# Column tiles for the attention value sums: prompt in two halves, sample in four quarters, and another place for the sample sums

## The chip, the cores and the metric

The kernel runs on one core of one Trainium2 chip. The metric is device time in microseconds. Three runs of the kernel before took 2574.14, 2576.84 and 2580.19 us; the median is 2576.84 us. One more execution was recorded by the hardware profiler.

The engines are called as the profile calls them: PE is TensorE (matmuls), PEld its weight loads, DVE is VectorE, ACT is ScalarE, POOL is GpSimd, and SP is the queue that issues most of the transfers. PSUM is the memory that matmuls write.

## The reference, cut to what matters

The program is one inference step of a two-layer decoder trunk. It serves a prompt of 1024 tokens and a sample group of 8 sequences with 8 new tokens each, which share all weights. Everything is fp32. Layer 0 joins a causal convolution with "stick-breaking" attention (8 heads of width 64); layer 1 joins a short convolution and a pooling; a SwiGLU block follows each.

The change touches only the end of the attention, the last line here:

```python
z = einsum('nqhd,nkhd->nhqk', qblk, k) * scale + bias_f
mask = k_pos[None, :] < pblk[:, None]
log_1m = where(mask, log_sigmoid(-z), 0.0)
after = cumsum(log_1m, reverse=True) - log_1m
wgt = exp(where(mask, log_sigmoid(z) + after, -inf))
out = einsum('nhqk,nkhd->nqhd', wgt, v)
```

For the prompt the keys are the prompt itself, so a query block of 128 tokens needs the key blocks up to its own. For the sample each of the 8 sequences has 8 pages of 128 past keys, found through a page table, and its 8 new keys.

## The kernel before, in words

**Main work and background work.** The order of instructions is written out by hand. The main work is the large matmuls of projections and SwiGLU (`mm3`, line 235: fp32r operands split into a high and a low part, three products). Between them stand slots; each slot calls `bg()` (line 341), which advances one background generator to its next `yield`. The attention and the convolution are such generators. One slot in the first SwiGLU is followed by 6 matmuls of 512 columns. Every engine takes its instructions in the order in which they were written.

**Tokens.** Prompt tokens 0 to 511 form group GA; prompt tokens 512 to 1023 and the 64 sample tokens form GB.

**Prompt attention** (`attention`, line 937) runs once for each group. Its units are pairs of head and query block: for GA the blocks 3, 2, 1, 0 of each head, for GB the blocks 7, 6, 5, 4. A unit passes four steps in four successive iterations of one loop (line 1029):

- s1: score matmuls into the PSUM tile `z2`, and two sigmoids on ACT (line 987).
- s2: on DVE two scans (lines 996 and 999) and a product (line 1001), which give the weights `be`.
- s3: PE transposes the weights, one 128x128 block per key block (line 1011), and ACT copies them into `wt` (line 1012).
- s4: the value sum. For key blocks 0 to i, a matmul adds a 64x128 product into one PSUM tile `o` (line 1020), and ACT copies it into the queries' place `qall` (line 1021).

An iteration u issues s4 of unit u-3, s3 of u-2, s2 of u-1, (in GB a slot,) s1 of u, then up to two small pieces that prepare the next head's keys and queries (lines 959 to 965), and a slot. The value rows `vrow` come from memory by one transfer a head (line 969).

**Sample attention** (`sample`, line 1051) takes two sequences at a time (`bp`, 4 of them). It has 48 steps: each handles half of the heads of up to three key pages. A step s transposes the key pages of step s+1 in two parts (`trans`, line 1104; PE line 1115, ACT line 1118, DVE line 1119), and multiplies the scores of step s (`score`, line 1128, line 1138). After the last page of a pair, the weights are made on DVE (lines 1163 to 1173) over the next three steps, then transposed in two parts (`weights_t`, line 1187): the first at once, the second through the list `soon`, and that of the new keys with the first value sum.

The value sums (`pv`, line 1202) wait in the list `pvq`, two pages of each sequence in one entry. The tile `o` has a half of 64 rows for each of the two sequences: 8 heads by 8 queries. A matmul with 64 weight columns adds all 512 value columns into such a half, so that each head's rows get the values of all heads; the useful blocks are picked at the end by `fin` with the selection matrix `sel` (line 1224). The value pages come by two transfers of 256 KB for each `pv` (line 597 through `page_to`); the tile `vst` has two buffers, so a page pair is loaded once the one two before it has been used.

In a step, the two parts of `trans` are separated by a `yield`; another `yield` stands before the scores, and a third at the end. An entry of `pvq` is taken after the scores in each even step, and in every step after the 48th.

**Two things at once in the sample stage.** `flow_c` (line 1358) interleaves `sample` with the second convolution `conv_b`: a `yield 1` of the sample attention leaves the convolution out, and of the other yields every second one advances it, by two DVE steps of 0.75 us.

Of the kernel before, what the change touches and what calls it, by code (L numbers as in the profile page):

```python
# [8 lines left out]
F = mybir.dt.float32  # L9
FR = mybir.dt.float32r  # L10
I32 = mybir.dt.int32
AF = mybir.ActivationFunctionType
OP = mybir.AluOpType
# [44 lines left out]
def trunk_kernel(ctx, tc, x_prompt, x_sample, cache_k, cache_v, state_conformer, state_shortconv, state_pool,  # L58
# [4 lines left out]
    pe, act, dve, pool, sp = nc.tensor, nc.scalar, nc.vector, nc.gpsimd, nc.sync  # L63
# [14 lines left out]
    def tmp():  # L78
        return tmpbox[0].tile([128, tmpbox[1]], F, name="tmp")
# [142 lines left out]
    def w_next(live=0):  # L222
        j = wj[0]
        wj[0] += 1
        w_split(j + 3 - live)
        w_load(need(j + 6 - live))
        return hls.pop(j)
# [411 lines left out]
    def ms():  # L639
        return mp.tile([128, 512], F, name="m")  # L640
# [5 lines left out]
    qall = hb[:, 4:8]  # L646
# [31 lines left out]
    m = ms()  # L678
# [258 lines left out]
    def attention(g):  # L937
# [3 lines left out]
        with ExitStack() as es_:  # L941
            pa = es_.enter_context(tc.tile_pool(name=f"pa{g.c0}", bufs=1))
            zp = es_.enter_context(tc.tile_pool(name=f"zp{g.c0}", bufs=1, space=PSUM, side="right"))
            op_ = es_.enter_context(tc.tile_pool(name=f"op{g.c0}", bufs=1, space=PSUM, side="right"))
# [4 lines left out]
            kt_, qa, vrow, small = {}, {}, {}, []  # L949
# [64 lines left out]
            def s4(u):  # L1014
                h, i = units[u]
                hp, hh = divmod(h, 2)
                w = wt.pop(u)
                o = op_.tile([64, 128], F, name="o2")
                for j in range(i + 1):
                    pe.matmul(o, vrow[h][:, j], w[:, j], start=j == 0, stop=j == i)  # L1020
                act.activation(qall[hh * 64:hh * 64 + 64, hp, i * 128:i * 128 + 128], o, AF.Copy)

            load_v(0)
            operands(0)
# [4 lines left out]
            for u in range(len(units) + 3):  # L1029
# [8 lines left out]
                if u < len(units):  # L1038
                    h, r = divmod(u, 4)
# [11 lines left out]
    def sample():  # L1051
# [5 lines left out]
        with ExitStack() as es_:  # L1057
            sa = es_.enter_context(tc.tile_pool(name="sa", bufs=1))
            zp = es_.enter_context(tc.tile_pool(name="zps", bufs=1, space=PSUM, side="right"))
            op_ = es_.enter_context(tc.tile_pool(name="ops", bufs=1, space=PSUM, side="right"))  # L1060
# [13 lines left out]
            for i in range(2):  # L1074
                r = slice(64 * i, 64 * i + 64)
                act.activation(sel[r, :, i], ident[r, r].rearrange("p (h x) -> p h x", h=4), AF.Copy)
            vnew = sa.tile([128, 512], F, name="vnew")
# [13 lines left out]
            vst, nv = {}, [0]  # L1091

            def load_v(upto):
                while nv[0] < min(upto, 32):
                    i = nv[0]
                    nv[0] += 1
                    bp, k = divmod(i, 8)
                    vst[i] = sa.tile([128, 2, 512], F, name="vst", bufs=2)
                    for b2 in range(2):
                        page_to(vst[i][:, b2], cache_v, (2 * bp + b2) * 8 + k)  # L1100
# [3 lines left out]
            def trans(u, pr, i):  # L1104
                bp, kb, b2 = units[u]
                n = (3, 3, 2)[kb]
                j = (2 * bp + b2) * 8 + 3 * kb
                if i == 0:
                    load_k(kpages.index(j) + n)
                    kth[u, pr] = sa.tile([128, 2, 2, 384], FR, name="kth", bufs=2)  # L1110
                t = kth[u, pr]
                if True:
                    m = ms()
                    for pg in range(n):
                        pe.transpose(m[:, pg * 128:pg * 128 + 128],
                                     kst[j + pg][:, (2 * pr + i) * 128:(2 * pr + i) * 128 + 128], ident)
                    h = t[:, 0, i, :n * 128]
                    act.activation(h, m[:, :n * 128], AF.Copy)
                    dve.tensor_tensor(t[:, 1, i, :n * 128], m[:, :n * 128], f32(h), op=OP.subtract)
                if i and pr:  # L1120
                    load_k(kpages.index(j) + n + KP)
                if i and kb == 2:
                    b = 2 * bp + b2
                    new = knew[:, 2 * pr:2 * pr + 2, 8 * b:8 * b + 8]
                    act.activation(t[:, 0, :, 256:264], new, AF.Copy)
                    dve.tensor_tensor(t[:, 1, :, 256:264], new, f32(t[:, 0, :, 256:264]), op=OP.subtract)

            def score(u, pr):
                bp, kb, b2 = units[u]
                if pr == 0:  # L1130
                    z[u] = zp.tile([128, 512], F, name="z")
                t = kth.pop((u, pr))
                n = NB[kb]
                for i in range(2):
                    hp = 2 * pr + i
                    q = qb[:, b2, hp * 128:hp * 128 + 128]
                    for s in range(2):
                        pe.matmul(z[u][:, :n], q, t[:, s, i, :n], start=hp == 0 and s == 0, stop=hp == 3 and s == 1)
# [19 lines left out]
            wx, wts, osum = {}, {}, {}  # L1158
# [34 lines left out]
            def turned(bp):  # L1193
                first, new = weights_t(bp)
                pvs = [lambda i=i: (pv(i), pv(i + 1)) for i in range(8 * bp, 8 * bp + 8, 2)]
                pvs[0] = lambda f=pvs[0]: (f(), new())
                soon.extend(first)
                pvq.extend(pvs)
# [3 lines left out]
            def pv(i):  # L1202
                bp, k = divmod(i, 8)
                if k == 0:
                    osum[bp] = op_.tile([128, 512], F, name="o")
                o = osum[bp]
                load_v(i + 1)
                for b2 in range(2):
                    r = slice(64 * b2, 64 * b2 + 64)
                    pe.matmul(o[r], wts[bp][:, k, r], vst[i][:, b2], start=k == 0, stop=False)  # L1210
                vst.pop(i)
                load_v(i + 3)
                if k < 7:
                    return
                for b2 in range(2):
                    r = slice(64 * b2, 64 * b2 + 64)
                    pe.matmul(o[r], wts[bp][:, 8, r], vnew, start=False, stop=True)
                ob = tmp()[:, 0:512]
                act.activation(ob, o, AF.Copy)

                def fin():
                    m = ms()
                    for hp in range(4):
                        pe.matmul(m[:, hp * 32:hp * 32 + 32], ob[:, hp * 128:hp * 128 + 128],
                                  sel[:, hp].rearrange("p b x -> p (b x)"), start=True, stop=True)
                    mv = m[:, 0:128].rearrange("p (h b y q) -> p h b y q", h=4, b=2, y=2)
                    c0 = SEQ + 16 * bp
                    for hh in range(2):
                        r = slice(hh * 64, hh * 64 + 64)
                        act.activation(qall[r, :, c0:c0 + 16].rearrange("p h (b q) -> p h b q", b=2),  # L1230
                                       mv[r, :, :, hh], AF.Copy)
                fins.append(fin)

            load_k(KP)
            steps = [(u, pr) for u in range(len(units)) for pr in range(2)]
            chain = {}
            pvq, soon = [], []
# [7 lines left out]
            s = 0  # L1245
            while s < len(steps) or chain or pvq or fins:
                todo = fins[:] + chain.pop(s, [])
                fins.clear()
                for f in todo:
                    f()  # L1250
                if s + 1 < len(steps):
                    trans(*steps[s + 1], 0)
                if s < len(steps):
                    yield 1 if todo else 2
                if s + 1 < len(steps):
                    trans(*steps[s + 1], 1)
                while soon:
                    soon.pop(0)()
                if s < len(steps):
                    yield 2  # L1260
                if s < len(steps):
                    u, pr = steps[s]
                    bp, kb, b2 = units[u]
                    score(u, pr)
                    if pr:
                        score_b(u)
                    if (kb, b2, pr) == (2, 1, 1):
                        if bp < 3:
                            fill_q(bp + 1)
                        w = weights(bp)  # L1270
                        for d, f in ((1, lambda w=w: next(w)), (2, lambda w=w: next(w)),
                                     (3, lambda bp=bp: weights_b(bp))):
                            chain.setdefault(s + d, []).append(f)
                        chain.setdefault(s + (4 if bp < 3 else 5), []).append(
                            lambda bp=bp: turned(bp))
                if pvq and (s % 2 == 0 or s >= len(steps)):
                    pvq.pop(0)()
                s += 1
                yield 2

# [372 lines left out]
    b2 = [xp.tile([128, 2, GB.n], FR, name=f"b2_{k}") for k in range(4)]  # L1653
# [67 lines left out]
    for n in range(2, KC):  # L1721
        h = w_next()
        a = accs()
# [4 lines left out]
    with tc.tile_pool(name="fab", bufs=1) as ep:  # L1728
        gen = forms_a(ep)
        for n in range(KC):  # L1730
            h = w_next()
            a = accs()
# [256 lines left out]
```

## Time and profile before

| What | us |
|---|---|
| Median of three runs | 2576.84 |
| Profiled execution | 2575.97 |
| Its span (first to last instruction) | 2574.2 |
| PE busy in it | 2477.7 |
| DVE busy in it | 1693.0 |
| ACT busy in it | 1105.3 |
| POOL busy in it | 1564.2 |
| Prompt value sums, first and last start | 238.2 and 563.7 |
| Sample value sums, first and last start | 679.4 and 924.4 |

Busy times overlap, since the engines run side by side. A row of a timeline gives the start, the length from the first start to the last end of the instructions merged in it, the engine, the line, the operation, the tile written and the tiles read, the shape and the count; then the idle time of the engine before it, and what ended that. A group row gives the busy time of the group and the mean length of one instruction, then idle time and what ended it. Matmuls are pipelined, so the length of one is longer than the distance of two starts.

### The profile page before, as it was taken

What the parts mean: (1) busy time and instruction counts of PE and PEld (TensorE: products, weight loads), DVE (VectorE), ACT (ScalarE), POOL (GpSimd) and SP (SyncE); (2) the same over time, 40 slices, a digit from 0 to 9 for tenths busy, and PEclk for the clock granted to TensorE, in tenths of its full rate; (3) what the DMA queues carried; (4) which work ended last, traced back from release to release, by engine and by line L of the source; (5) the groups of instructions that cost most, each with busy time, mean ns of one, the idle gap of its engine ahead of it and who ended that gap; (6) DMA issues with size and microseconds to landing.
All of it is one profiled execution on the core that took longest, in us unless ns stands there. A gap on an engine that the chain in (4) does not pass through costs nothing.

```text
span 2574.2 us, 41142 instructions
## 1 busy us (share of the span) xinstructions
PE 2477.7 (96%) x15727; PEld 2213.7 (86%) x15727; DVE 1693.0 (66%) x2359; ACT 1105.3 (43%) x1875; POOL 1564.2 (61%) x1205
## 2 busy tenths in 40 slices
PE   8999999999999999999999999999999998999998
PEld 6788877887777668989999889989888887999997
DVE  3696777968867734467666633348776778666655
ACT  5536766754444334334333522234434434443333
POOL 6754243544434346678777722266888885887775
PEclk9999999999999999999999999999999999999999
DMA  7342231224555434222323411152233332333322
GB/s 220 113 113 74 64 109 46 70 83 142 157 162 160 139 107 152 74 74 83 99 83 98 130 42 46 38 161 65 84 91 96 95 96 82 107 95 103 99 83 78
DMA packets 355484, 258.30 MB, mean 100 GB/s; under 512 B 22913, under 2 KB 303617, under 8 KB 355272
## 3 DMA queue, kind: packets, MB, share of 16 engines
q1 hardware_dynamic: 355256, 255.66, 33.8%
q8 instruction: 125, 2.05, 0.3%
q14 instruction: 71, 0.58, 0.1%
q10 hardware_dynamic: 32, 0.01, 0.0%
HBM read 237.41 MB, written 18.69 MB: 99 GB/s over the span
## 4 chain that ended last, share of the span: by engine, by line
PE 44%; DVE 8%; POOL 2%; issue 1%; ACT 1%; POOLq 0%; DVEq 0%; ACTq 0%
PE acc L235 23%; PE acc L521 20%; POOL hl L197 1%; DVE sum L200 1%; DVE hid L241 1%; DVE hb L295 1%; DVE sum L201 1%; DVE b L1669 0%; DVE tmp L525 0%; DVE sum L202 0%; DVE x L1669 0%; DVE sum_c L214 0%; DVE fb L1673 0%; DVE xs L1673 0%; POOL tmp L500 0%
## 5 line engine op out<-in xcount | busy, mean ns | idle before, releaser
L186 POOL TENSOR_TENSOR hl<-stage,hl 128x512 fp32r<-128x512 f32 x464 | 634.7, 1391 | 475.1 <-ACT hl L184 357.0
L235 PE MATMUL acc<-x,hl 128*128 128x512 f32 (+1 forms) x3648 | 780.6, 350 | 12.2 <-DVE hb L295 2.6
L235 PEld LDWEIGHTS acc<-x,hl 128*128 128x128 f32 x3648 | 581.4, 189 | 77.2 <-issue 10.9
L235 PE MATMUL acc<-hid,hl 128*128 128x288 f32 (+1 forms) x3096 | 552.3, 334 | 16.8 <-DVE hb L295 6.9
L235 PEld LDWEIGHTS acc<-hid,hl 128*128 128x128 f32 x3096 | 470.4, 190 | 69.9 <-DVE hb L295 11.0
L295 DVE TENSOR_TENSOR hb<-acc,hb 128x512 f32<-128x512 f32 (+1 forms) x360 | 256.4, 718 | 184.8 <-PE acc L235 183.4
L521 PE MATMUL acc<-x,hl 128*128 128x288 f32 (+1 forms) x2676 | 362.4, 290 | 6.0 <-ACT x L1792 2.0
L521 PEld LDWEIGHTS acc<-x,hl 128*128 128x128 f32 x2676 | 349.0, 188 | 8.4 <-POOL hl L197 2.7
L197 POOL TENSOR_TENSOR hl<-sum,hl 128x512 fp32r<-128x512 f32 x180 | 237.1, 1344 | 168.6 <-ACT hl L196 168.5
L184 ACT ACTIVATE hl<-stage 128x1024 fp32r<-128x1024 f32 x232 | 243.5, 1055 | 218.5 <-PE acc L235 129.6
L525 DVE TENSOR_TENSOR tmp<-acc,tmp 128x288 f32<-128x288 f32 (+1 forms) x420 | 173.5, 441 | 228.0 <-ACT tmp L537 135.3
L197 POOL TENSOR_TENSOR hl<-stage,hl 128x512 fp32r<-128x512 f32 x180 | 267.0, 1505 | 13.3 <-ACT hl L196 13.3
L521 PE MATMUL acc<-b,hl 128*128 128x256 f32 (+1 forms) x1548 | 216.6, 291 | 14.1 <-DVE tmp L525 11.2
L521 PEld LDWEIGHTS acc<-b,hl 128*128 128x128 f32 x1548 | 202.3, 189 | 19.6 <-ACT hl L196 12.7
L235 PE MATMUL acc<-x1t,hl 128*128 128x288 f32 x1152 | 216.4, 296 | 1.5 <-POOL hl L186 1.5
L235 PEld LDWEIGHTS acc<-x1t,hl 128*128 128x128 f32 x1152 | 196.0, 188 | 19.4 <-POOL hl L186 1.7
L196 ACT ACTIVATE hl<-sum 128x512 fp32r<-128x512 f32 x180 | 103.1, 623 | 237.9 <-DVE sum L202 217.6
L291 DVE TENSOR_TENSOR tmp<-acc,rr 128x512 f32<-128x512 f32 (+1 forms) x108 | 75.0, 709 | 113.2 <-PE acc L235 100.0
L500 POOL TENSOR_TENSOR tmp<-tmp 128x576 f32<-128x576 f32 (+1 forms) x85 | 127.8, 1504 | 11.7 <-ACT tmp L477 8.3
L196 ACT ACTIVATE hl<-stage 128x512 fp32r<-128x512 f32 x180 | 105.6, 618 | 67.5 <-PE acc L235 62.3
L241 DVE TENSOR_TENSOR hid<-tmp,hid 128x512 fp32r<-128x512 f32 (+1 forms) x88 | 99.1, 1127 | 44.0 <-ACT hid L240 41.2
L235 PE MATMUL acc<-x1a,hl 128*128 128x512 f32 x480 | 121.7, 407 | 2.5 <-POOL hl L186 1.3
(289 smaller groups left out, 3242.9 us busy)
## 6 DMA issues: line engine op xcount, KB each, us to landing
stage<-in_w_ffn_in_dram SPq DMA_DIRECT2D x176, 512.0 KB
stage<-in_w_ffn_out_dram SPq DMA_DIRECT2D x88, 512.0 KB
stage<-in_w_in_even_dram SPq DMA_DIRECT2D x40, 512.0 KB
kst<-in_cache_k_dram SPq DMA_DIRECT2D x64, 256.0 KB
vst<-in_cache_v_dram SPq DMA_DIRECT2D x64, 256.0 KB
stage<-in_w_out_even_dram SPq DMA_DIRECT2D x16, 512.0 KB
stage<-in_w_in_odd_dram SPq DMA_DIRECT2D x16, 512.0 KB
stage<-in_w_out_odd_dram SPq DMA_DIRECT2D x16, 512.0 KB
```

The source lines that it names most:

```text
L184: act.activation(hl[:, 0], st, AF.Copy)
L186: pool.tensor_tensor(hl[:, 1, c], st[:, c], f32(hl[:, 0, c]), op=OP.subtract)
L196: act.activation(hl[:, 0, c], x, AF.Copy)
L197: pool.tensor_tensor(hl[:, 1, c], x, f32(hl[:, 0, c]), op=OP.subtract)
L200: todo = [lambda: dve.tensor_tensor(sb, su[:, lo], su[:, hi], op=OP.add), lambda: dve.tensor_tensor(sa[:, hi], sg[:, lo], su[:, lo], op=OP ...
L235: pe.matmul(acc[:, b, :c1 - c0], w, xs[:, xi, c0 - o:c1 - o], start=first and s == 0, stop=last and s == 2)
L241: (on or dve).tensor_tensor(dst[:, 1], src, f32(dst[:, 0]), op=OP.subtract)
L291: dve.tensor_tensor(d, a, r, op=OP.mult)
L295: dve.tensor_tensor(d, a, d, op=OP.add)
L500: (dve if both and f == NF - 1 else pool).tensor_tensor(t[:, :n], t[:, :n], u[:, :n], op=OP.mult)
L521: pe.matmul(acc[:, :w2], h[:, wi, i, k], xk[:, xi], start=k == 0 and s == 0, stop=k == 3 and s == 2)
L525: dve.tensor_tensor(out, acc[:, :w2], x, op=OP.add)
```

## The change

In the prompt attention, the tile `o` gets 128 rows. The matmuls of even key blocks add into rows 0 to 63, those of odd key blocks into rows 64 to 127. Where there is more than one key block, ACT copies the upper half into a new tile `ot`, and DVE adds the lower half to it and writes the result; with one key block, ACT copies the lower half as before.

In the sample attention, each 64-row half of `o` becomes two quarters of 32 rows (four heads each), and a matmul for a quarter takes only the 256 value columns of its four heads. `o` becomes 256 columns wide, and so does the copy of it.

In the steps of the sample attention, an entry of `pvq` is taken between the two parts of `trans`, in odd steps (and in every step after the 48th), and not while `soon` holds something. The `yield` between the two parts of `trans` is kept only in steps that had other things to do first; otherwise it moves behind the second part.

```diff
-                o = op_.tile([64, 128], F, name="o2")
+                o = op_.tile([128, 128], F, name="o2")
                 for j in range(i + 1):
-                    pe.matmul(o, vrow[h][:, j], w[:, j], start=j == 0, stop=j == i)
-                act.activation(qall[hh * 64:hh * 64 + 64, hp, i * 128:i * 128 + 128], o, AF.Copy)
+                    pe.matmul(o[j % 2 * 64:j % 2 * 64 + 64], vrow[h][:, j], w[:, j], start=j < 2, stop=j >= i - 1)
+                r = slice(hh * 64, hh * 64 + 64)
+                a = qall[r, hp, i * 128:i * 128 + 128]
+                if i == 0:
+                    act.activation(a, o[0:64], AF.Copy)
+                    return
+                t = pa.tile([128, 128], F, name="ot", bufs=2)
+                act.activation(t[r], o[64:128], AF.Copy)
+                dve.tensor_tensor(a, o[0:64], t[r], op=OP.add)
...
-                    osum[bp] = op_.tile([128, 512], F, name="o")
+                    osum[bp] = op_.tile([128, 256], F, name="o")
...
-                for b2 in range(2):
-                    r = slice(64 * b2, 64 * b2 + 64)
-                    pe.matmul(o[r], wts[bp][:, k, r], vst[i][:, b2], start=k == 0, stop=False)
+                for t in range(4):
+                    r, c = slice(32 * t, 32 * t + 32), slice(256 * (t % 2), 256 * (t % 2) + 256)
+                    pe.matmul(o[r], wts[bp][:, k, r], vst[i][:, t // 2, c], start=k == 0, stop=False)
...
-                for b2 in range(2):
-                    r = slice(64 * b2, 64 * b2 + 64)
-                    pe.matmul(o[r], wts[bp][:, 8, r], vnew, start=False, stop=True)
-                ob = tmp()[:, 0:512]
+                for t in range(4):
+                    r, c = slice(32 * t, 32 * t + 32), slice(256 * (t % 2), 256 * (t % 2) + 256)
+                    pe.matmul(o[r], wts[bp][:, 8, r], vnew[:, c], start=False, stop=True)
+                ob = tmp()[:, 0:256]
...
-                        pe.matmul(m[:, hp * 32:hp * 32 + 32], ob[:, hp * 128:hp * 128 + 128],
+                        pe.matmul(m[:, hp * 32:hp * 32 + 32], ob[:, hp % 2 * 128:hp % 2 * 128 + 128],
...
                     trans(*steps[s + 1], 0)
-                if s < len(steps):
-                    yield 1 if todo else 2
+                if pvq and not soon and (s % 2 or s >= len(steps)):
+                    pvq.pop(0)()
+                if todo and s < len(steps):
+                    yield 1
                 if s + 1 < len(steps):
                     trans(*steps[s + 1], 1)
                 while soon:
                     soon.pop(0)()
                 if s < len(steps):
+                    if not todo:
+                        yield 2
                     yield 2
...
-                if pvq and (s % 2 == 0 or s >= len(steps)):
-                    pvq.pop(0)()
                 s += 1
                 yield 2
```

## The prediction

> **What bounds the kernel now.** I read the page first, its totals and its slices.
>
> ```profile
> span 2574.2 us, 41142 instructions
> PE 2477.7 (96%) x15727; PEld 2213.7 (86%) x15727; DVE 1693.0 (66%) x2359; ACT 1105.3 (43%) x1875; POOL 1564.2 (61%) x1205
> PE   8999999999999999999999999999999998999998
> DVE  3696777968867734467666633348776778666655
> ```
>
> TensorE is busy in every slice, so a matmul taken away shortens the run unless another engine then sets the pace. Slices 4 to 15 (64.4 us each) hold what the change touches, and there VectorE's digits go up to 9. So I asked for the stages: prompt attention of the first token half, of the second half, one head of the latter, sample attention, and its tail.
>
> ```profile
> core 0: us, PE busy (x) PEld busy (x) DVE busy (x) ACT busy (x) POOL busy (x), PEclk, DMA share, GB/s
> 238.25:337.10 98.85, 96.61 (x691) 85.05 (x690) 69.56 (x104) 67.90 (x156) 25.68 (x46) 1.00 0.22 60
> 359.00:564.00 205.00, 199.70 (x1164) 162.67 (x1164) 167.79 (x154) 134.85 (x217) 90.71 (x82) 1.00 0.21 58
> 474.39:498.33 23.94, 23.94 (x144) 19.74 (x143) 20.88 (x19) 16.88 (x28) 9.59 (x12) 1.00 0.20 55
> 565.00:900.00 335.00, 319.37 (x1560) 245.14 (x1558) 258.99 (x427) 136.44 (x281) 141.22 (x108) 0.99 0.53 155
> 900.00:930.00 30.00, 26.32 (x89) 11.70 (x90) 6.05 (x10) 6.45 (x13) 4.98 (x4) 0.94 0.50 140
> ```
>
> TensorE ends last in all of them, but in the second-half head VectorE works 20.88 of 23.94 us: it has 3.06 us of room for a whole head. In the sample stage it has 76 us of room in 335, and there the main work binds through TensorE alone.
>
> **Prompt value sums: what is removed.** The groups by shape give counts and prices.
>
> ```profile
> L1020 PE MATMUL o<-wt,vrow 128*64 128x128 f32 x576 | 76.6, 278 | 0.0
> L1210 PE MATMUL o<-vst,wts 128*64 128x512 f32 x128 | 39.3, 657 | 3.0 <-DMA vst<-in_cache_v_dram 1.6 <-ACT wts L1188 1.3
> L1217 PE MATMUL o<-vnew,wts 128*64 128x512 f32 x16 | 5.0, 596 | 0.0
> L1021 ACT ACTIVATE hb<-o 64x128 f32<-64x128 f32 x64 | 17.0, 266 | 35.6 <-PE o L1020 35.2
> L1149 DVE TENSOR_TENSOR zs<-z,zs 64x384 f32<-64x384 f32 x16 | 8.7, 546 | 4.4 <-ACT zs L1148 4.2
> ```
>
> An fp32 matmul leaves two records: 288 matmuls (8 heads x (4+3+2+1) and 8 x (8+7+6+5)) make 576. The mean of 278 ns is a latency; the pace is read off the timeline of TensorE.
>
> ```profile
> 480.60 1.74 PE L1020 MATMUL o<-wt,vrow 128*64 128x128 f32 x14
> 482.27 0.88 PE L1011 MATMUL m<-ident,be 128*128 128x128 f32 x6
> 492.57 1.31 PE L1020 MATMUL o<-wt,vrow 128*64 128x128 f32 x10
> 493.81 1.09 PE L1011 MATMUL m<-ident,be 128*128 128x128 f32 x8
> ```
>
> 14 records take 1.67 us to the next line's start, 10 take 1.24: 0.108 us each and about 0.15 of entry and exit, which stay. Whether two column halves run at once is shown by the sample sums, which use halves already:
>
> ```profile
> 721.11 0.64 PE L1138 MATMUL z<-kth,qb 128*128 128x264 f32 x4
> 721.68 0.20 PEld L1210 LDWEIGHTS o<-vst,wts 128*64 128x64 f32 x4
> 721.68 1.94 PE L1210 MATMUL o<-vst,wts 128*64 128x512 f32 x8
> 722.16 0.14 PEld L1210 LDWEIGHTS o<-vst,wts 128*64 128x64 f32 x2 [0.28 <-issue]
> 723.45 1.03 PE L1217 MATMUL o<-vnew,wts 128*64 128x512 f32 x4
> 724.41 1.66 PE L235 MATMUL acc<-x,hl 128*128 128x512 f32 x6
> ```
>
> Eight records of 512 columns take 1.77 us, 0.22 each; at the pace of the 128-column ones alone (0.108 x 4) one would take 0.43. So halves do run in pairs, and their weight loads come in pairs too (two in 0.14 us). With pairs, n matmuls take the time of n/2 rounded up: 4, 3, 2, 1 become 2, 2, 1, 1 (4 fewer a head) and 8, 7, 6, 5 become 4, 4, 3, 3 (12 fewer). Each is two records, 0.217 us: first half 8 x 4 x 0.217 = 6.9 us, second half 8 x 12 x 0.217 = 20.8, together 27.7.
>
> [...]
>
> **Prompt: what is added.** ScalarE's copy stays one of 64x128 (0.266 us), now of the upper half. New is a VectorE add for 56 of the 64 units. No add of 64x128 is in the trace; the 64x384 add from PSUM takes 0.546, the copy of this very shape on ScalarE 0.266, so between these; I take 0.28, near the copy, since the size is the same: 56 x 0.28 = 16 us of VectorE. Four a head make 1.1 us of the 3.06 of room, while TensorE takes 2.6 out of the head: 23.94 - 2.6 = 21.3 against 20.88 + 1.1 = 22.0. So VectorE becomes the bound by its work alone and 0.7 of the 2.6 is lost.
>
> More is lost to order. The add stands on VectorE ahead of the next unit's scans (line 996), and waits for ScalarE's copy, which waits in its own queue. A second-half head, by ScalarE, VectorE and TensorE:
>
> ```profile
> 511.60 1.05 ACT L959 ACTIVATE kt<-kall 64x1024 fp32r<-64x1024 f32 x1
> 512.56 0.61 ACT L960 ACTIVATE qa<-hb 64x512 fp32r<-64x512 f32 x1
> 513.08 0.25 ACT L1021 ACTIVATE hb<-o 64x128 f32<-64x128 f32 x1
> 510.60 1.54 DVE L996 TENSOR_TENSOR_SCAN q<-q,ident 128x128 f32<-128x128 f32 x1 [1.14 <-ACT q L987]
> 514.39 1.23 DVE L1001 TENSOR_TENSOR be<-be,q 128x1023 f32<-128x1023 f32 x1
> 517.74 1.09 PE L1011 MATMUL m<-ident,be 128*128 128x128 f32 x8
> ```
>
> The copy (behind the next head's key and query copies) ends at 513.33; the scan that now starts at 510.60 will start after it and the add, 3.0 us later. Its product, ready at 515.62, is needed by the transposes at 517.74: 2.1 us of slack, less the 1.1 that two shortened sums take out before it. That is 2.0 us of new TensorE wait in a head that saves 2.6; behind the scans stand VectorE's key subtractions and accumulator reads, so the following unit is late too. Such a head keeps almost nothing. First half:
>
> ```profile
> 277.37 0.41 DVE L996 TENSOR_TENSOR_SCAN q<-q,ident 128x128 f32<-128x128 f32 x1
> 278.22 0.27 ACT L1021 ACTIVATE hb<-o 64x128 f32<-64x128 f32 x1 [0.52 <-PE o L1020]
> 279.47 1.23 DVE L1001 TENSOR_TENSOR be<-be,q 128x255 f32<-128x255 f32 x1
> 281.23 0.44 PE L1011 MATMUL m<-ident,be 128*128 128x128 f32 x2
> ```
>
> Here the scan goes from 277.37 to 278.3 at the earliest (the copy comes 0.4 sooner, the add follows): 1.0 late against a slack of 281.23 - 280.70 = 0.5. Ends: the first half keeps 0 to 6.9, the second 0 to 20.8 less the 0.7 x 8. Not every head is like these two; nearer to the zero they show, I take 2 and 7: **9 us**.
>
> **Sample value sums.** A page pair's sum is now two pairs of 512-column records, 2 x 0.43 = 0.86 us (the 1.77 is two sums with the entry); it becomes 8 records of 256 columns in four quarters. No 32-column tile is in the trace. Ends: all four at once, 2 x 0.215 = 0.43; two at a time, 0.86; one after the other, 1.72. Halves run fully in pairs, so I take 0.44: 0.42 saved, for 24 sums and 3 closing ones before the tail: **11.3 us**. The evacuation (line 1219) halves, off the path. [...]
>
> **One fp32 clump.** The pop of the value sums moves from behind the scores to between the two transposes of the next step. Its page loads on SP's queue move with it, still ahead of that step's second key load, and each waits for its sum as before. From L1138 to L1210 TensorE takes 721.68 - 721.11 = 0.57 for four records that were issued at about 0.12, so some 0.1 is lost on entry. The new neighbours, full-width transposes, still change the column width; so between 0 and 12 clumps x 0.1 = 1.2 I take less than half, **0.5 us**. The slots for main work per step stay three. The convolution's VectorE pieces cover the two adjacent transposes' reads; if VectorE were full, each step could cost the 0.55 of such a read.
>
> **Tail.** The last eight sums:
>
> ```profile
> 900.68 1.09 PE L1187 MATMUL m<-ident,bet 128*128 128x128 f32 x8 [2.65 <-DVE bet L1173]
> 903.04 3.49 PE L1210 MATMUL o<-vst,wts 128*64 128x512 f32 x8 [1.27 <-ACT wts L1188]
> 905.08 14.28 SPq L597 DMA_DIRECT2D vst<-in_cache_v_dram  x12
> 923.07 0.64 PE L1210 MATMUL o<-vst,wts 128*64 128x512 f32 x1 [0.98 <-DMA vst<-in_cache_v_dram]
> 924.93 1.66 PE L235 MATMUL acc<-x,hl 128*128 128x512 f32 x6
> ```
>
> The first pop now comes one step after its weights, so main work covers the 1.27 us wait; the 2.65 stays. From 905 the value pages set the pace, and halved matmuls only free buffers a little sooner. Ends 1 and 7; I take 1.3 + 1.7 = **3 us**.
>
> **Sum.** 9 + 11.3 + 0.5 + 3 = 23.8. The profiled execution took 2575.97 us (span 2574.2); 2552.2 from it, and the median of the runs, 2576.84, lies 0.9 above: 2553.
>
> **Rivals.**
> A: the adds cost nothing, because VectorE and ScalarE have more slack elsewhere. For it: only 4 units a head, and TensorE waited little for line 1001 until now. Against: 20.88 of 23.94. 27.7 + 11.3 + 0.5 + 3 = 42.5: 2534.
> B: quarters run two at a time. Nothing excludes it in the trace. 9 + 0 + 0.5 + 1.5 = 11: 2566.
> C: at 128 columns the halves don't overlap, since a load of 0.136 us no longer fits under a stream of 0.108. Prompt then -3 (adds without a gain): 11.8 saved, 2565. [...]
> D, slower: the adds' wait ahead of line 996 falls on TensorE each time. From 42.5 / 56 = 0.76 us per add it eats all gains. At the delays of the two heads (1.3 for 24 adds, 3.0 for 8, 0.28 for 24) it would be 62 us: 19 slower, 2596. Against: slacks of 0.5 and 2.1 in the same rows.
>
> **Chances.** Forecast 50, A 17, B 12, C 11, D 5; no change to be told 5. The likeliest's own range is 2543 to 2562 (prompt 0 to 18). With A, B and C inside, 2533 to 2569. A measurement of this kernel tells about 0.2% (5 us) from no change: faster 0.89, same 0.05, slower 0.06.
>
> **What would show it.** L1020: the x14 clump at about 1.0 us instead of 1.67 (C: unchanged). L1210: eight records in 0.44 us, their loads in fours (B: 0.86). New TensorE waits "L1011 <- DVE L1001" of 10 to 20 us (A: under 5; D: over 45). The wait of 1.27 us for line 1188 gone. The prediction is wrong if such waits come from elsewhere, above all if adjacent transposes make TensorE wait for line 1119.

## The result, and the profile after

The changed kernel takes 2585.01 us (median of five runs, 2583.41 to 2590.14) against 2576.84: a ratio of 1.0036, 95% interval 1.0021 to 1.0050. It is slower by about 9 us; 24 us faster had been forecast. The page of its profiled execution:

```profile
span 2581.6 us, 41528 instructions
PE 2443.3 (95%) x15871; PEld 2194.4 (85%) x15871; DVE 1706.5 (66%) x2415; ACT 1106.4 (43%) x1875; POOL 1566.6 (61%) x1205
PE   8999888889999989999999999999999999999998
DVE  3696777787888845467666733347777778667655
```

TensorE has 34.4 us less work than before (2477.7), and the span is 7.4 us longer. The slices with an 8 for PE (5 to 9, where the kernel before has 9) are the prompt attention. So the matmul time was saved, and more than that came back as waiting. Stage by stage, first the changed kernel (prompt sums, sample stage), then the one before, each from the first prompt sum:

```profile
239.47:583.00 343.53, 297.88 (x1940) 241.94 (x1937) 265.83 (x332) 223.94 (x403) 124.04 (x136) 0.97 0.23 64
583.00:916.00 333.00, 311.63 (x1685) 249.20 (x1685) 267.99 (x435) 139.01 (x288) 140.81 (x109) 0.99 0.53 156
```

```profile
238.25:563.95 325.70, 315.67 (x1941) 262.45 (x1940) 253.78 (x277) 221.58 (x402) 123.09 (x136) 1.00 0.24 67
563.95:903.00 339.05, 321.51 (x1572) 246.87 (x1571) 261.95 (x432) 139.51 (x287) 141.78 (x109) 0.99 0.52 153
```

The columns are window, length, then busy time of PE, PEld, DVE, ACT and POOL, granted clock, DMA share, GB/s. The prompt stage grew by 17.8 us; the sample stage to the first sum of its tail shrank by 6.1. In the prompt stage TensorE was not busy for 325.7 - 315.7 = 10.0 us before and for 45.7 after. The table of waits says for whom. TensorE's wait for VectorE's product, first in the kernel before, then in the changed kernel:

```profile
PE m L1011 <- DVE be L1001: 3.0, 3, 1.6
```

```profile
PE m L1011 <- DVE be L1001: 38.1, 33, 3.7
```

VectorE's wait in the changed kernel:

```profile
DVE hb L1028 <- ACT ot L1027: 42.1, 28, 2.7
```

The columns are total, times and longest. TensorE's transposes (line 1011) waited 3.0 us in all for VectorE's product before, and 38.1 now. VectorE in turn stood 42.1 us in front of the new add (line 1028) until ScalarE had copied the upper half (line 1027). The groups by shape show what the parts cost:

```profile
L1020 PE MATMUL o<-wt,vrow 128*64 128x128 f32 x576 | 48.9, 283 | 0.7 <-ACT wt L1012 0.7
L1217 PE MATMUL o<-vst,wts 128*32 128x256 f32 x256 | 21.4, 391 | 5.8 <-DMA vst<-in_cache_v_dram 5.0 <-ACT wts L1195 0.7
L1028 DVE TENSOR_TENSOR hb<-o,ot 64x128 f32<-64x128 f32 x56 | 15.8, 282 | 42.6 <-ACT ot L1027 42.1
L1027 ACT ACTIVATE ot<-o 64x128 f32<-64x128 f32 x56 | 15.3, 273 | 20.5 <-PE o L1020 19.0
```

The prompt sums take 48.9 us instead of 76.6, so 27.7 less, as predicted; that even the tenth agrees is chance. The add takes 0.282 us (0.28 predicted). The rest is waiting. Two places of the prompt stage, TensorE's timeline:

```profile
366.51 1.09 PE L1020 MATMUL o<-wt,vrow 128*64 128x128 f32 x16
370.03 1.73 PE L1011 MATMUL m<-ident,be 128*128 128x128 f32 x7 [2.42 <-DVE be L1001]
514.28 1.09 PE L1020 MATMUL o<-wt,vrow 128*64 128x128 f32 x16
517.68 0.96 PE L1011 MATMUL m<-ident,be 128*128 128x128 f32 x7 [2.31 <-DVE be L1001]
```

Sixteen records now take 1.09 us (14 took 1.74 before), and then TensorE stands for 2.4 and 2.3 us. The seven transposes that follow take 1.73 us in the first place and 0.96 in the second: at 370 the clock was halved. The first two of the stretches in which it was, and the sum of all five:

```profile
369.70:373.10 3.40, 3.07 (x11) 2.81 (x12) 3.30 (x5) 1.07 (x2) 3.04 (x3) 0.50 0.45 108
397.00:400.40 3.40, 3.40 (x12) 2.91 (x11) 3.20 (x5) 1.07 (x2) 0.00 (x0) 0.50 0.01 2
...
sum 20.40, PE 18.50 PEld 16.17 DVE 17.91 ACT 6.70 POOL 9.70; mean PE 3.70 PEld 3.23 DVE 3.58 ACT 1.34 POOL 1.94
```

So 20.4 us of the prompt stage ran at a granted clock of 0.50, where the stage's clock before was 1.00. Half of the 18.5 us of matmuls in these windows, 9.2 us, is an estimate of what that cost. Inside this stage the waits for line 1001 were 37.0 us, and 3.0 before (the rest of the 38.1 stands ahead of its first sum). The stage's account is then: 27.7 us of matmuls saved, 34.0 more waited for VectorE, 9.2 lost at half clock: 15.5 longer, of 17.8 measured.

The account also holds in each half. To 344.90 us (first token half, clock 1.00) 6.9 us were saved and the waits grew by 11.0 (12.4 after 1.4); the stretch is 6.5 us longer. From there on 21.0 us were saved, the waits grew by 23.0 (24.6 after 1.6) and the half clock cost 9.2: 11.2, of 11.4 measured. So in both halves the new waits alone are more than the gain.

That the waits bring the half clock is what the trace suggests; no run sets out to show it. The waits that end at the start of the five stretches or just inside them are 2.42, 2.78, 2.62, 3.52 and 3.66 us long. The five stretches last 3.41 us each, the fourth 6.83, and start at 369.70, 397.00, 448.20, 465.30 and 543.80 us, whole multiples of 3.41 us apart (8, 15, 5 and 23 of them). Cut by this step, the stage has these rows in the 3.41 us ahead of the first and the last stretch, and in the two windows that share the wait of 2.31 us before 517.68, which brought no half clock:

```profile
366.29:369.70 3.41, 1.32 (x18) 0.85 (x16) 3.31 (x2) 2.66 (x5) 3.41 (x2) 1.00 0.67 187
540.39:543.80 3.41, 0.00 (x0) 0.00 (x0) 3.38 (x3) 0.11 (x1) 2.36 (x1) 1.00 0.54 154
513.04:516.45 3.41, 2.33 (x22) 1.59 (x20) 3.38 (x2) 2.54 (x4) 3.41 (x2) 1.00 0.00 0
516.45:519.86 3.41, 2.18 (x13) 1.96 (x14) 3.31 (x5) 0.98 (x2) 0.18 (x2) 1.00 0.55 158
```

TensorE was busy for 0.39, 0.18, 0.28, 0.38 and 0.00 of the window ahead of each of the five, and for 0.54 or more of every window of the stage at full clock that none followed. So in this trace the half clock came where a wait had left TensorE busy for 0.39 of one such window or less; the wait of 2.31 us, which falls across two windows (busy for 0.68 and 0.64), had none behind it. Four of the five stretches follow a wait for line 1001. The third, at 448.20, follows one of 2.62 us for line 382, which stands in the kernel before too (2.59 us), without a half clock behind it; so some 7.6 of the 9.2 us come behind the new waits. In the trace of `prompt_only`, below, the split is not as clean: one window at 0.55 was followed by the half clock, one at 0.44 was not.

### The profile page after: what moved, and what is told of

Same layout as the page of the kernel before. It is cut to its first block, busy times and chain, and to the rows that moved or that the text cites. A ratio compares the mean times of both kernels' runs of the same rounds, so it can differ in the third digit from the quotient of the medians.

```text
span 2581.6 us, 41528 instructions
## 1 busy us (share of the span) xinstructions
PE 2443.3 (95%) x15871; PEld 2194.4 (85%) x15871; DVE 1706.5 (66%) x2415; ACT 1106.4 (43%) x1875; POOL 1566.6 (61%) x1205
## 4 chain that ended last, share of the span: by engine, by line
PE 43%; DVE 8%; POOL 2%; issue 1%; ACT 1%; POOLq 0%; DVEq 0%; ACTq 0%
PE acc L235 23%; PE acc L521 19%; POOL hl L197 2%; DVE sum L200 1%; DVE hid L241 1%; DVE hb L295 1%; DVE sum L201 1%; DVE sum L202 0%; DVE b L1678 0%; DVE x L1678 0%; POOL tmp L500 0%; DVE tmp L525 0%; DVE fb L1682 0%; DVE xs L1682 0%; PE blk L1901 0%
## 5 line engine op out<-in xcount | busy, mean ns | idle before, releaser
L521 PE MATMUL acc<-b,hl 128*128 128x256 f32 (+1 forms) x1548 | 216.3, 291 | 13.9 <-DVE tmp L525 11.2
```

Source lines behind the costliest of these rows:

```text
L521: pe.matmul(acc[:, :w2], h[:, wi, i, k], xk[:, xi], start=k == 0 and s == 0, stop=k == 3 and s == 2)
```

## The experiments

Two theories. **W**: the loss is an order. The add stands at the head of VectorE's queue and waits for ScalarE's copy; the scans behind it start late, and the transposes after them. **V**: the loss is work. VectorE had 3 us of room in a head and cannot take 16 us more. Beside them stood the question whether the sample part pays at all. All ratios are to the kernel before, with 95% intervals; differences in us are worked out from the ratios.

### The two parts alone

`sample_only` is the changed kernel with the old function `s4`; `prompt_only` is the kernel before with the new one:

```diff
# sample_only, against the changed kernel; prompt_only is the reverse, against the kernel before
-                o = op_.tile([128, 128], F, name="o2")
+                o = op_.tile([64, 128], F, name="o2")
                 for j in range(i + 1):
-                    pe.matmul(o[j % 2 * 64:j % 2 * 64 + 64], vrow[h][:, j], w[:, j], start=j < 2, stop=j >= i - 1)
...
+                    pe.matmul(o, vrow[h][:, j], w[:, j], start=j == 0, stop=j == i)
+                act.activation(qall[hh * 64:hh * 64 + 64, hp, i * 128:i * 128 + 128], o, AF.Copy)
```

> The prompt attention as in the kernel before; the sample quarters and the moved pop as in the changed kernel. Theory W (the loss is in the prompt part alone: VectorE's add waits for ScalarE at the head of VectorE's queue, ahead of the scans): 8 to 14 us faster than before, 2563 to 2569, and TensorE's wait for line 1001 stays at about 3 us. Rival S (the sample part does not pay either: its waits for key reads and pages give its gain back): within 5 us of before, 2572 to 2582.

> The prompt halves with VectorE's add as in the changed kernel; the sample attention as in the kernel before. Theory W: 15 to 20 us slower than before, 2592 to 2597, with some 38 us of TensorE waits for line 1001. Rival S: the prompt part costs 8 us or less, 2585 or below.

Measured: `sample_only` 2565.87 us, ratio 0.9959 (0.9943 to 0.9975), 11 us faster. `prompt_only` 2593.94 us, ratio 1.0073 (1.0053 to 1.0093), 19 us slower, with 37.0 us of waits for line 1001. The sum of the two, +8, is the change's own +9. The sample part pays, and the prompt part loses.

### The wait without the work, and the work without the wait

Both leave all sums as in the kernel before and add one VectorE instruction at the place of the add:

```diff
# wait_alone
-                act.activation(qall[hh * 64:hh * 64 + 64, hp, i * 128:i * 128 + 128], o, AF.Copy)
+                r = slice(hh * 64, hh * 64 + 64)
+                a = qall[r, hp, i * 128:i * 128 + 128]
+                act.activation(a, o, AF.Copy)
+                if i:
+                    dve.tensor_copy(a[:, 0:1], a[:, 0:1])
# work_alone
+                if i:
+                    t = pa.tile([128, 128], F, name="ot", bufs=2)
+                    dve.tensor_tensor(t[0:64], ones[0:64], ident[0:64], op=OP.add)
```

> The kernel before in all its sums, and one more VectorE instruction of a single column (64x1, a copy onto itself of what ScalarE has just written) at the place of the add for the 56 units with more than one key block. It has the wait on ScalarE's copy and next to no work. Theory W: the scans are held back as in the changed kernel; since TensorE gives up no time here, the slack of each unit is larger: 10 to 30 us slower than before, 2587 to 2607, and 15 us or more of TensorE waits for line 1001. Rival V: under 4 us slower, below 2581.

> The kernel before in all its sums, and at the place of the add, for the same 56 units, one VectorE add of 64x128 whose inputs are two constants that have long been ready. It has the work of the add and no wait. Theory W: next to nothing, under 4 us slower than before, and TensorE's wait for line 1001 stays under 8 us. Rival V (added work where VectorE has little room): 8 us slower or more, with the wait for line 1001 above 15 us.

Measured: `wait_alone` 2587.24 us, ratio 1.0047 (1.0029 to 1.0064), 12 us slower. `work_alone` 2576.31 us, ratio 1.0006 (0.9996 to 1.0015), no difference that could be told. The waits of `wait_alone`, first TensorE's:

```profile
PE m L1011 <- DVE be L1001: 12.7, 14, 2.2
```

then VectorE's, at the new instruction (line 1025), for ScalarE's copy:

```profile
DVE hb L1025 <- ACT hb L1023: 48.8, 33, 2.9
```

TensorE's wait in `work_alone`:

```profile
PE m L1011 <- DVE be L1001: 5.3, 4, 1.6
```

and the group of its add, from the groups by shape:

```profile
L1024 DVE TENSOR_TENSOR ot<-ones,ident 64x128 f32<-64x128 f32 x56 | 33.1, 591 | 0.1
```

The instruction of one column that waits is dear here: its 56 copies take 8.2 us of work. 33.1 us more of VectorE's time, twice what the real add takes, cost nothing that could be told (-1 to +4 us). So V falls as the cause, as far as TensorE keeps its old pace. W holds. The 12.7 us of TensorE's waits here are a third of the changed kernel's 38.1, probably since in `wait_alone` TensorE's own pace is unchanged and the units keep their slack.

The mean of 0.591 us hides two kinds of adds. 37 of the 56 took 0.27 to 0.28 us; the other 19, up to 1.38 us, each began while a `TENSOR_TENSOR` of GpSimd was running and ended 0.14 to 0.15 us after it (two of the 37 overlapped with one as well). One of the 19, with the row of GpSimd:

```profile
254.18 2.71 POOL L186 TENSOR_TENSOR hl<-stage,hl 128x512 fp32r<-128x512 f32 x2 [0.86 <-DVE q L999]
255.66 1.37 DVE L1024 TENSOR_TENSOR ot<-ones,ident 64x128 f32<-64x128 f32 x1
```

In the changed kernel, where one input of the add lies in PSUM, 21 of the 56 adds ran beside such an operation and none took over 0.288 us.

### The add behind the scans

```diff
# late_add
-                dve.tensor_tensor(a, o[0:64], t[r], op=OP.add)
+                return lambda: dve.tensor_tensor(a, o[0:64], t[r], op=OP.add)
...
                 if 1 <= u < len(units) + 1:
                     s2(u - 1)
+                if fin:
+                    fin()
# late_free: late_add, and PSUM is emptied by ScalarE alone
                 act.activation(t[r], o[64:128], AF.Copy)
+                act.activation(a, o[0:64], AF.Copy)
+                return lambda: dve.tensor_tensor(a, a, t[r], op=OP.add)
```

> The changed kernel, with the same add of the halves written behind the scans and the product of the next unit on VectorE instead of ahead of them. Theory W: the work is the same, but the scans no longer wait for ScalarE's copy, so TensorE's wait for line 1001 falls from 38 to under 12 us, and the kernel is 20 to 35 us faster than the changed one, 2550 to 2565. Rival V (VectorE's added work of 16 us in a stage where it has little room sets the pace): the waits stay above 25 us and the time above 2575.

> As the kernel with the late add, but ScalarE copies both halves out of PSUM (56 copies of 64x128 more), and VectorE adds them from SBUF, still behind the scans. The PSUM tile is then free without VectorE. Theory W2 (with the late add TensorE's next sum waits for the single PSUM tile that the late add holds, 11 us for VectorE and 8 us for ScalarE in that run): the wait of line 1020 for VectorE goes, and the kernel is 6 to 14 us faster than with the late add, 2548 to 2557. Rival A (ScalarE's queue is what is late): no gain, 2560 or above.

Measured: `late_add` 2562.49 us, ratio 0.9943 (0.9925 to 0.9961); `late_free` 2557.07 us, ratio 0.9924 (0.9908 to 0.9941). With the same instructions in another order the changed kernel is 24 us faster; W is confirmed, and V falls for a faster TensorE too. But `late_add` has only 4 us more than the sample part alone, of 27.7. Its waits of TensorE:

```profile
PE o L1020 <- DVE hb L1028: 11.3, 9, 2.2
PE o L1020 <- ACT qa L964: 6.4, 4, 1.7
PE m L1011 <- DVE be L1001: 2.6, 2, 2.4
```

The wait of line 1011 is gone, 2.6 us as before the change. In its place the sums themselves (line 1020) wait for the single PSUM tile, which the add now holds until the scans are through. Emptying it by ScalarE takes that wait away and gains 5 us, but `late_free` still waits:

```profile
PE m L1011 <- DVE be L1001: 18.1, 16, 3.3
```

Its adds read both inputs from SBUF, and 18 of the 56 took 0.84 us or more behind GpSimd, so that they hold VectorE for 32.9 us instead of 15.8. Whether the 18.1 us of waits come from that was not tried.

### Halves without an add

The two halves need no add if each has its own columns of the result: the first 64 queries and the last 64, over all key blocks.

```diff
# query_halves
-                o = op_.tile([128, 128], F, name="o2")
+                o = op_.tile([128, 64], F, name="o2")
                 for j in range(i + 1):
-                    pe.matmul(o[j % 2 * 64:j % 2 * 64 + 64], vrow[h][:, j], w[:, j], start=j < 2, stop=j >= i - 1)
...
+                    for t in range(2):
+                        pe.matmul(o[64 * t:64 * t + 64], vrow[h][:, j], w[:, j, 64 * t:64 * t + 64],
+                                  start=j == 0, stop=j == i)
+                for t in range(2):
+                    c = i * 128 + 64 * t
+                    act.activation(qall[hh * 64:hh * 64 + 64, hp, c:c + 64], o[64 * t:64 * t + 64], AF.Copy)
```

> The sample part as in the changed kernel. In the prompt the two column halves take the first and the last 64 queries of a block, each over all key blocks, so that no add is needed: twice as many matmuls of 64 columns, two copies of 64x64 on ScalarE, nothing on VectorE. Theory W: nothing new stands ahead of the scans, and the prompt gives some 15 to 26 us on top of the sample part: 2540 to 2552. Rival L (weight loads set the pace of so short matmuls, so 64 columns take as long as 128): the prompt gives nothing, 2563 to 2572.

> The kernel before with the prompt sums in two halves of 64 queries (no add), the sample part as before. Theory W: the halves are worth what TensorE gives up, 27.7 us, less the slack of the scans that it takes: 13 to 21 us faster than before, 2553 to 2561. Rival: most of the gain of the run with both came from the two parts together; then under 10 us.

Measured: `query_halves` 2548.49 us, ratio 0.9896 (0.9880 to 0.9913), 27 us faster than the kernel before; `query_prompt_only`, which has these halves and the old sample part, 2556.63 us, ratio 0.9937 (0.9921 to 0.9954), 16 us faster. A row of TensorE's timeline of `query_halves`, the same 16 sums as 32 records:

```profile
487.38 1.15 PE L1021 MATMUL o<-wt,vrow 128*64 128x64 f32 x32
```

The groups by shape of the sums and of their copies:

```profile
L1021 PE MATMUL o<-wt,vrow 128*64 128x64 f32 x1152 | 47.6, 227 | 0.0
L1025 ACT ACTIVATE hb<-o 64x64 f32<-64x64 f32 x128 | 27.7, 216 | 19.9 <-PE o L1021 17.7
```

And TensorE's wait for the scans:

```profile
PE m L1011 <- DVE be L1001: 11.8, 14, 2.4
```

Twice as many records, with twice as many weight loads (1152 of 137 ns, 576 of 136 in the changed kernel), take the same time (47.6 against 48.9), so rival L falls. ScalarE has 10.7 us more to do than the 17.0 of the kernel before, and nothing new stands before the scans. The sums are 29.0 us shorter, and 16 arrive (12 to 20 by the interval). In `query_halves` TensorE's waits for the scans are 8.8 us more than the 3.0 before, and the half clock came for three windows of 3.41 us in the prompt stage (two in `query_prompt_only`), some 5 us in `query_halves` by the same estimate. The prediction has neither term: without the add, its 21.3 us of TensorE in a head stand against 20.88 of VectorE, which leaves no loss. What makes VectorE late there was not tried.

### The sample part's two edits

`clump_only` is the kernel before with the moved pop and the moved stop; `quarters_only` is the kernel before with the quarters alone; `query_old_pop` is `query_halves` with the loop of the kernel before. Their diffs are those parts of the change, as shown.

> The kernel before with the moved pop and the moved stop alone: the sample sums in two halves of 512 columns, the prompt as before. By the prediction's term the tail's 1.3 us of wait and some 0.5 us of entries: 0 to 4 us faster, 2571 to 2575. Rival: adjacent transposes make TensorE wait for the reads of their PSUM tiles (line 1119) and the kernel is 3 us slower or more.

> The kernel before with the sample sums in four quarters of 256 columns, popped where they were, the prompt as before. If the pop's place is worth nothing (it was alone), this has the whole gain of the sample part: 6 to 12 us faster than before, 2562 to 2569. Rival: quarters and moved pop need each other (the tail), then 3 us or less.

> Query halves in the prompt and quarters in the sample, with the pop and its stop where they were in the kernel before. If the pop's place is worth nothing: as fast as the run with the moved pop, 2545 to 2552. If the moved pop gives the tail's 1.3 us and more: 2551 to 2555.

Measured: `clump_only` 2575.03 us, ratio 1.0004 (0.9994 to 1.0013); `quarters_only` 2563.91 us, ratio 0.9957 (0.9940 to 0.9974); `query_old_pop` 2548.74 us, ratio 0.9895 (0.9879 to 0.9912). The quarters are the whole gain of the sample part, and the pop's place is worth nothing that could be told, alone or with the quarters. TensorE's timeline at a sum that closes a pair, in the changed kernel:

```profile
739.20 1.07 PE L1217 MATMUL o<-vst,wts 128*32 128x256 f32 x16
740.09 0.61 PE L1224 MATMUL o<-vnew,wts 128*32 128x256 f32 x8
740.63 0.55 PE L1122 MATMUL m<-ident,kst 128*128 128x128 f32 x3
```

Sixteen records of two sums take 0.89 us (1.77 before), so four quarters run at once. TensorE's waits of `sample_only` in this stage:

```profile
PE m L1115 <- DVE kth L1119: 5.4, 3, 2.6
PE o L1210 <- DMA vst<-in_cache_v_dram: 4.2, 6, 1.4
...
PE m L888 <- DVE kth L1119: 2.8, 2, 1.9
```

and those of the kernel before, there:

```profile
PE m L1115 <- DVE kth L1119: 4.8, 4, 2.4
PE o L1210 <- DMA vst<-in_cache_v_dram: 1.6, 3, 1.0
```

TensorE waits 2.6 us more for value pages and 2.8 us for key reads ahead of line 888, which did not wait before. The first comes with the quarters (4.8 us in `quarters_only`), the second with the moved pop and stop (2.7 us in `clump_only`, none in `quarters_only`). The moved pop also covers some waits: in `clump_only` that of line 1210 for line 1188 fell from 1.3 to 0.7 us and that of line 1187 for line 1173 from 2.7 to 1.2, which the wait of line 888 takes back.

## Why the prediction was wrong

**Halves and quarters on TensorE: right.** 27.7 us of prompt sums, forecast and measured; pairs at 128 columns (48.9 us instead of 76.6), fours at 256 (0.89 us for two sums instead of 1.77). Rivals B and C fall.

**The add's price: right.** 0.282 us against 0.28, taken near one end of 0.266 to 0.546.

**The add's place: the step that failed.** The prediction named the mechanism: "The add stands on VectorE ahead of the next unit's scans (line 996), and waits for ScalarE's copy". It worked out two heads and found that such a head "keeps almost nothing". Then it gave the ends as "the first half keeps 0 to 6.9, the second 0 to 20.8", and took 2 and 7. The lower end of zero has no argument: the stall worked out for one unit was never multiplied by the number of units. In the first half it was 0.5 us for an add (1.0 late against a slack of 0.5); times 24 adds that is 12 us, against 6.9 saved, and 11.0 were measured. In the second half it was 2.0 us a head for one unit, 16 us for eight heads, with "the following unit is late too" left without a price; 23.0 were measured, against 20.8 saved. `prompt_only` measured -19 where the sum had +9, and this 28 us is nearly all of the error of 32. What the runs showed in its place is 34 us of new TensorE waits in the prompt stage, and about 9 us at half clock, a term which the sum did not have at all.

**Rival D had the right direction, with 5 in 100.** It has the adds' wait fall on TensorE each time, 62 us of delays without any slack. Its own sign, waits over 45 us, did not come: there were 38.1, 35.1 more than before, between it and the forecast's 10 to 20. That it gives 19 us slower and the prompt part alone lost 19 is chance: its 19 is for the whole change, which lost 9. The 62 is also too high by its own rows: it takes 1.3 us for the first half's 24 adds, where the working above gave 1.0; with that it is 55, and 12 slower. Its break-even, 0.76 us per add, was nearly met by the waits alone (35.1 / 56 = 0.63). Rival A (no cost) falls by `prompt_only`.

**VectorE's work as a bound: not what cost the change.** "VectorE becomes the bound by its work alone and 0.7 of the 2.6 is lost" would be 5.6 us in eight heads. `work_alone`, at TensorE's old pace, costs nothing that could be told; in `late_add`, with the faster TensorE and the same adds, the waits for line 1001 are 2.6 us.

**Sample sums: right.** 11.3 for the quarters; `quarters_only` is 11 us faster (7 to 15), tail included. Two sums take 0.89 us, so one takes the 0.44 of the sum.

**Clump and tail: not seen.** 0.5 and 3 us were given; `clump_only` measured -0.06% to +0.13%, from 1.5 us faster to 3.3 slower. The tail was also read wrongly: the wait of 1.27 us, which main work was to cover, fell only to 0.7, the one of 2.65, which was to stay, fell to 1.2, and 2.7 us of new waits at line 888 came in their place, although the convolution's pieces were to cover such reads. Of the tail's remainder nothing was measured by itself.

## What to carry to other kernels

Before an instruction is added to a queue, look at what it waits for and at what stands behind it: here one column's worth of work at the head of VectorE's queue cost 12 us, and twice the add's VectorE time without the wait cost nothing that could be told. If column tiles are to share a sum, split the columns of the result rather than the contraction, so that no add is needed; where an add is needed, put it behind the work that the next stage waits for, and see who holds the PSUM tile meanwhile. When a hand calculation gives a stall for one place, multiply it by the number of such places before the range is set: here that gave 12 us lost against 6.9 gained, and a range that ended at zero could not hold it.

## What the runs showed of the hardware that was not expected

Four column quarters of fp32 run at once: 16 records of 256 columns in 0.89 us, where two halves of 512 took 1.77 for 8. Pairs of 64 columns keep the rate of pairs of 128: 47.6 us for 1152 records, 48.9 for 576.

A VectorE add of 64x128 with both inputs in SBUF was held up by GpSimd: 19 of 56 in `work_alone` took 0.47 to 1.38 us, each begun under a `TENSOR_TENSOR` of GpSimd and ended 0.14 to 0.15 us after it; the others took 0.28. With one input in PSUM, 21 adds of the changed kernel ran beside GpSimd at 0.28 us.

In the changed kernel's prompt stage the clock of 0.50 came in four stretches of 3.41 us and one of 6.83, which start whole multiples of 3.41 us apart, each behind a window in which TensorE was busy for 0.39 of the time or less; behind the windows at full clock with 0.54 or more it did not come (`prompt_only` has an exception each way, at 0.55 and 0.44). The prompt stage before the change had no such window; `sample_only` and `work_alone`, whose prompt sums are those of the kernel before, had one each, behind the wait for line 382.
